# The recurrence head weights' parts in the general tile pool, begun half a slot ahead, and the copies of x moved from the opening to the conv part

## The chip, the core and the metric
One core of a Trainium2 chip. The metric is the device time of one execution in microseconds (us). The kernel before took 731.68 us, the median of three runs from 730.69 to 732.34 us. The profiled execution is a run of its own, with its own time.

## The reference
One layer of a decoder trunk for a sequence of 1024 tokens with 1024 channels, all in fp32:

```python
h = rmsnorm(x, norm_g[l]) * (1.0 + scale[:, None, :]) + shift[:, None, :]
u = h @ w_in[l]                       # conv value, conv gate, conv SiLU gate, lru x, lru gate
v = causal_depthwise_conv(cv * jax.nn.sigmoid(cg), dw_w[l], dw_b[l])      # 31 taps
v = jax.nn.silu(layernorm(v, cln_g[l], cln_b[l]))
y_conv = (v @ pw2_w[l] + pw2_b[l]) * jax.nn.silu(cs)
xs = causal_depthwise_conv(lx, sc_w[l], sc_b[l])                          # 4 taps
...                                   # gates r and i, a, bx: a linear recurrence along the tokens
hs = linear_scan(a, bx)
y_lru = hs * jax.nn.silu(ls)
y = jnp.concatenate([y_conv, y_lru], axis=-1) @ w_out[l]
x = x + (1.0 + gate[:, None, :]) * y
return rmsnorm(x, final_g)
```

shift, scale and gate come from c through a matrix mod_w. `w_out` has 2048 rows: the first 1024 take y_conv, the last 1024 take y_lru. In what follows "lru weights" are those last rows.

## The kernel before, in words
Channels lie on the 128 partitions, tokens along the free axis, so each tensor is eight tiles of 128 x 1024 fp32 (512 KB). A product in fp32 is made from three in the fast fp32r format: an operand w is split in `hi`, its rounded copy, and `lo`, the rest, and the product is hi·hi + hi·lo + lo·hi. Every weight therefore passes three steps before TensorE may use it: a load into a buffer `raw` (SP's queue), a rounding copy `whi` on ScalarE (line 373), and `wlo`. For weights of the early slots `wlo` is a subtraction on GpSimd or VectorE (line 400). For the lru weights it is `remainder` (line 488): ScalarE writes minus `whi` into `wlo` (line 381), and a DMA from GpSimd's queue adds the weight from DRAM onto it (`ADD`, line 403).

The work of TensorE is a row of **slots** n, one per 128 output columns. Slots 4 to 39 are columns of w_in (48 matmuls of 128 x 512 each, written to `ps`, line 525), with eight small gate products between them. Slots 40 to 45 are the lru part of w_out in three **pairs** (`lru_pair`, line 1337): two columns together by a scheme with seven half-size products and the rest straight, with seven letters in `LORDER` for its order. Its matmuls write `lp`, `lx` and `ly` (lines 525 and 1370). Slots 46 and 47 are the last two lru columns, made straight. After them come pw2 (`xpw`, `zpw`, `ypw`, line 694) and the y_conv half of w_out (`xout` and others).

Buffers of 128 x 1024 come from pools. The general pool `big` has NBIG = 47 of them. `raw`, `whi` and `wlo` have pools of their own with two buffers each (lines 345 and 346): a third weight's `whi` has to wait until the first one's matmuls are done. `w_bufs` (line 504) picks the pools.

Nothing is ordered by hand. Every operation is entered in a `Plan` (line 144) with an engine, an estimated cost, the buffers that it reads and writes, and a priority, which for most work is the slot number less or plus something: weights load at n - 2.5 and are prepared at n - 1.4. `Plan.order` (line 206) plays the program through with these costs, and gives each free engine the ready operation of the lowest number whose buffers can be had. The order that comes out is then the program of each engine's queue, and the chip runs each queue in order. An operation with `reserve` is only taken when so many buffers of `big` stay free beside those it needs. `after` orders the plan alone: on the chip only the data's own dependencies are waited for.

The steps that the change and the prediction touch:

- `split` (line 1193) of the recurrence's outputs: `yh` by ScalarE, `yl` by VectorE, priority 38 + 0.2 i, `reserve` SPARE + 1 = 6 for `yh` and 5 for `yl`. They need buffers of `big`, and those come free in slot 39, the last that reads the layer's inputs `uh` and `ul` (two for each of its eight steps k).
- `lru_sums` (line 1267): sums and differences of pairs of those outputs for the scheme, `yhs` and `yls`, at priority 38 + 0.4 j + LTP.
- `lru_prepare` (line 1293): in the opening, sums of lru weights for the scheme (`lz`), made with accumulating DMAs from GpSimd's queue and stored in DRAM.
- `x_copy` (line 1323): nine DMAs from SP's queue that copy x within DRAM to `accd`, 4 MB in all, where the lru part's products are later added (`acc_store`, line 1334, GpSimd's queue). They are entered when n is PREN = 5, with priority XCP = 19.
- `conv_pooled` (line 1126): the depthwise conv of three tiles as a chain of accumulating DMAs from GpSimd's queue (`es<-cq`, `oo<-co`), fed by ScalarE.

Of the kernel before, what the change touches and what calls it, by code (L numbers as in the profile page):

```python
# [14 lines left out]
P = 128  # L15
D = 1024
T = 1024
KT = D // P
# [69 lines left out]
LK = tuple(2 * j + z for z in (0, 1) for j in JS) + tuple(k for k in range(KT) if k // 2 not in JS)  # L88
LACT = ((0, 0), (0, 1), (1, 0), (1, 1))
LORDER = "p1zy2q3s4r"  # L90
LTP = 0.2
LTD = (2,1)
PREN, PRES = 5, 3
PREP, XCP = 18, 19
LEV = ()
QRES = 0
SINGLE = (0,)
AHEAD = 4
# [12 lines left out]
LATE, LAND = 41, 6.0  # L111
# [32 lines left out]
class Plan:  # L144
# [14 lines left out]
    @staticmethod  # L159
    def keys(items):  # L160
        for it in items:
            if isinstance(it, tuple):
                yield it
            else:
                for i in range(it.parts):
                    yield (it, i)
# [162 lines left out]
def hymba_layer(ctx: ExitStack, tc: tile.TileContext, xT, vecs, mod_w, w_first, w_in,  # L329
# [73 lines left out]
    def ADD(prio, out, a, n=T, r=(), w=(), after=(), flight=FLIGHT):  # L403

        return S.op("POOL", ISSUE, lambda: pool.dma_start(out(), a(), accum_op=ALU.add), prio, r,  # L405
                    w, lag=RATE * n / T, after=after, flight=flight)
# [10 lines left out]
    def DMA(prio, out, in_, nbytes, r=(), w=(), after=(), reserve=0):  # L417
        return S.op("SP", max(0.1, nbytes / 360e3),
                    lambda: sp.dma_start(out(), in_()), prio, r, w, after=after,
                    reserve=reserve)  # L420
# [57 lines left out]
    def wsrc(s):  # L478
        if s[0] == "in":
            return w_in[s[1]]  # L480
        if s[0] == "lru":
            return w_out[KT + s[1]]
        return w_out[s[1]] if s[0] == "out" else pw2[s[1]]

    def k3(b):
        return lambda: b().rearrange("p (k c) -> p k c", k=KT)

    def remainder(prio, lo, hi, src, n, rk, wk, sk=(), reserve=0):
        ACT(prio, lo, lambda: hi().bitcast(F32), AF.Copy, n, scale=-1.0, r=rk, w=wk, reserve=reserve)
        ADD(prio, lo, src, n, r=[*wk, *sk], w=wk, flight=LAND)  # L490
# [13 lines left out]
    def w_bufs(s, where=None):  # L504
        n = number[s]
        raw[s] = S.buf("raw", f"raw{n}", F32, KT)
        if where == "all":
            raw[s] = S.buf("big", f"raw{n}", F32, KT)
        whi[s] = S.buf("big" if where else "whi", f"whi{n}", F32R, KT)
        wlo[s] = S.buf("big" if where else "wlo", f"wlo{n}", F32R, KT)  # L510

    def weights(s, after=(), n=None, eng=None, where=None, late=()):
        n = number[s] if n is None else n
        eng = eng or ("DMA" if n in EARLYD or n >= LATE else "POOL" if n < EARLY else "DVE")
        w_bufs(s, where)
        w_slice(s, 0, KT, n - 2.5, n - 1.4, after, eng, late)
# [776 lines left out]
    def lru_prepare(p, after):  # L1293
        w_ = NJ * P
        s0, s1 = wsrc(("lru", 2 * p)), wsrc(("lru", 2 * p + 1))
        z, sh, sl = big_buf(f"lz{p}", parts=4), big_buf(f"lh{p}", F32R), big_buf(f"ll{p}", F32R)

        def block(i):
            return part(z, i * w_, i * w_ + w_)

        def src(w, i):
            return lambda: w[:, i * NJ:i * NJ + NJ, :].rearrange("p k c -> p (k c)")
        load = lambda i, w, k, **kw: DMA(PREP, block(i), src(w, k), P * w_ * 4, w=[(z, i)], after=after, **kw)
        add = lambda i, w, k: ADD(PREP, block(i), src(w, k), w_, r=[(z, i)], w=[(z, i)], flight=LAND)

        def minus(i, k):
            ACT(PREP, block(i), block(k), AF.Copy, w_, scale=-1.0, r=[(z, k)], w=[(z, i)])
        load(3, s1, 0, reserve=PRES)
        minus(0, 3)
        add(0, s0, 0)  # L1310
        add(3, s1, 1)
        minus(2, 0)
        add(2, s1, 1)
        minus(1, 2)
        add(1, s0, 1)
        ACT(PREP, sh, z, "copy", r=[z], w=[sh])
        ACT(PREP, sl, lambda: sh().bitcast(F32), AF.Copy, scale=-1.0, r=[sh], w=[sl])
        ADD(PREP, sl, z, r=[z, sl], w=[sl], flight=LAND)
        for h, t in zip("hl", (sh, sl)):
            s_d[h, p] = dram.tile([P, T], F32, tag=f"ls{h}{p}", name=f"lsd{h}{p}")  # L1320
            DMA(PREP, lambda h=h: s_d[h, p], lambda t=t: t().bitcast(F32), FULL_BYTES, r=[t], w=[("ls", h, p)])
# [15 lines left out]
    def lru_pair(p, n, use, firsts):  # L1337
        rest = LK[2 * NJ:]
        s0, s1 = ("lru", 2 * p), ("lru", 2 * p + 1)
        q = n - 1.4  # L1340
        for s in (s0, s1):
            w_bufs(s)
            DMA(n - 2.5, k3(raw[s]), lambda s=s: wsrc(s)[:, :, :], FULL_BYTES, w=[raw[s]])
        r0, r1 = raw[s0], raw[s1]
        for s, k in ((s0, 0), (s1, NJ)):
            hi, lo, r = whi[s], wlo[s], raw[s]
            cut = lambda b, k=k: (lambda: k3(b)()[:, k:, :])
            keys = lambda b, k=k: [(b, i) for i in range(k, KT)]
            ACT(q, cut(hi), cut(r), "copy", (KT - k) * P, r=keys(r), w=keys(hi))
            remainder(q, cut(lo), cut(hi), lambda s=s, k=k: wsrc(s)[:, k:, :], (KT - k) * P, keys(hi), keys(lo))  # L1350
        def kk(b, i):
            return [(b, k) for k in range(i * NJ, i * NJ + NJ)]

        sh, sl = (big_buf(f"ls{h}{p}", F32R) for h in "hl")
        for h, t in zip("hl", (sh, sl)):
            DMA(n - 2.2, lambda t=t: t().bitcast(F32), lambda h=h: s_d[h, p], FULL_BYTES, r=[("ls", h, p)], w=[t], after=firsts)
        wq = {"S3": (sh, sl, 0, 0), "S4": (sh, sl, 1, 0), "S2": (sh, sl, 2, 0), "S1": (sh, sl, 3, 0),
              "A11": (whi[s0], wlo[s0], 0, None), "A12": (whi[s0], wlo[s0], 1, None),
              "A22": (whi[s1], wlo[s1], 1, None)}
        p0, x, y = mm_tile(f"lp{p}"), mm_tile(f"lx{p}"), acc_tile(f"ly{p}")  # L1360
        g, ops = 0.0, {}

        def quarter(c, a, b, ps, h, begin):
            wh, wl, i, key = wq[a]
            rk = [(wh, key), (wl, key)] if key is not None else kk(wh, i) + kk(wl, i)
            for j, (bh, bl) in enumerate(lsets[b]):
                def emit(j=j, bh=bh, bl=bl):
                    o = (i * NJ + j) * P
                    for lhs, rhs, t in ((wh, bh, 0), (wh, bl, 1), (wl, bh, 2)):
                        pe.matmul(half(ps, h)(), lhs()[:, o:o + P], half(*rhs)(),  # L1370
                                  start=begin and j == 0 and t == 0, stop=j == NJ - 1 and t == 2,
                                  skip_group_check=True)
                o = S.op("PE", 3 * (H + 32) / 2400, emit, n + g, [*rk, bh, bl],
                         [(ps, h if ps.parts > 1 else 0)], columns=3 * H)
                ops.setdefault(c, o)

        for c in LORDER:
            g += 0.12
            if c == "p":
                for k in rest:  # L1380
                    o = mm_k(n + g, p0, s0, yh, yl, k, FULL, first=rest[0])
                    ops.setdefault(c, o)
            elif c == "q":
                for k in rest:
                    mm_k(n + g, y, s1, yh, yl, k, FULL[1:], off=H, first=-1)
                use(n, 1, 1, half(y, 0), (y, 0))
            elif c == "r":
                for k in rest:
                    mm_k(n + g, x, s1, yh, yl, k, FULL[:1], first=-1)
                use(n, 1, 0, half(x, 0), (x, 0))  # L1390
            else:
                a, b, ps, h, begin, i, z = {
                    "1": ("A11", "B11", x, 0, True, 0, 0), "z": ("A12", "B21", p0, 0, False, 0, 0),
                    "2": ("S2", "T2", x, 0, False, 0, 1), "3": ("S3", "T3", x, 0, False, 1, 1),
                    "y": ("S1", "T1", y, 0, True, 0, 1), "s": ("S4", "B22", p0, 1, False, 0, 1),
                    "4": ("A22", "T4", x, 0, False, None, 0)}[c]
                quarter(c, a, b, ps, h, begin)
                if i is not None:
                    use(n, i, z, half(ps, h), (ps, h if ps.parts > 1 else 0))
        return ops["p"], ops["2"]  # L1400
# [67 lines left out]
    for s in slots[4:]:  # L1468
# [23 lines left out]
            n += 1  # L1492
            continue
        if s not in NEXT:
            weights(s, late=[pending_evac[n]] if n in pending_evac else ())
        if GM <= n < GM + 8:
            gate_mod(n - GM, n, [started[n - 2]] if n - 2 in started else [])
        m = s[1]
# [13 lines left out]
        if n == PREN:  # L1512
            for p in range(LRU_P):
                lru_prepare(p, [started[n]])
            for i in range(KT):
                x_copy(i, [started[n]])
        if s[0] == "in":
# [214 lines left out]
```

## Time and profile before

| | before |
|---|---|
| median of 3 runs | 731.68 us |
| profiled execution, its time | 734.07 us |
| its span, first to last instruction | 732.30 us |
| TensorE busy | 719.3 us |
| VectorE, ScalarE, GpSimd busy | 619.9, 479.3, 170.0 us |
| TensorE clock granted, mean | 0.996 |

The profile's page gives each engine's busy time, the span in 40 slices, the chain of work that ended last, and the costliest groups. Besides the page the trace answers to views: who waited for whom, the instructions of one engine in order of time, busy times by stretch of the span, and the DMA queues. In a row of the timeline stand the start and the duration in us, the engine, the line, the operation, what it writes and reads, and in brackets the idle time just before with what ended it. Buffer numbers are left out: `wlo` stands for every weight's rest.

### The profile page before, as it was taken

To read this page: it belongs to the slowest core of one execution; us is meant where nothing else is said; L and a number is where in the kernel's file an instruction comes from. 1 tells how busy PE (TensorE), PEld (TensorE's weight loads), DVE (VectorE), ACT (ScalarE), POOL (GpSimd) and SP (SyncE) were. 2 spreads that over 40 slices of the span, in tenths; PEclk is the share of its full clock that TensorE was granted. 3 is DMA by queue.
4 is the path that set the end of the run, shared out by engine and by line. 5 is a ranking of instruction groups with operands and counts; after the bars stand their busy time and mean duration, and the time that the engine had idled before them with its cause. 6 is when DMAs were issued, how large, how long until landed. Compare 5 with 4: busy or idle time off the path is not lost.

```text
span 732.3 us, 9063 instructions
## 1 busy us (share of the span) xinstructions
PE 719.3 (98%) x3274; PEld 597.4 (82%) x3274; DVE 619.9 (85%) x848; ACT 479.3 (65%) x614; POOL 170.0 (23%) x172
## 2 busy tenths in 40 slices
PE   9999999999999999999999999999999999999996
PEld 8888878888888888888888888787877888888885
DVE  7999999999789998688499995998897556999646
ACT  7650589565689767957949869757793345755322
POOL 0035223343534230233220220111111001010003
PEclk9999999999999999999999999999999999999998
DMA  9946838758898997899893695998577845784006
GB/s 340 407 154 204 240 102 232 200 116 200 181 221 201 266 234 200 183 226 207 191 198 73 134 208 137 265 247 213 108 142 157 230 118 132 219 216 181 15 15 215
DMA packets 46059, 137.80 MB, mean 188 GB/s; under 512 B 5200, under 2 KB 15824, under 8 KB 45904
## 3 DMA queue, kind: packets, MB, share of 16 engines
q0 software_dynamic: 20016, 54.84, 41.8%
q1 hardware_dynamic: 24992, 81.48, 31.9%
q10 hardware_dynamic: 1008, 0.92, 0.4%
q8 instruction: 25, 0.41, 0.2%
q14 instruction: 18, 0.15, 0.1%
HBM read 79.37 MB, written 21.50 MB: 138 GB/s over the span
## 4 chain that ended last, share of the span: by engine, by line
PE 74%; DVE 11%; DMA 6%; ACT 4%; issue 3%; SPq 0%; POOL 0%; DVEq 0%; ACTq 0%; POOLq 0%
PE ps L525 38%; PE xout L694 6%; PE xpw L694 6%; PE first L821 5%; PE ypw L694 3%; PE gate L1241 3%; DMA lz<-in_w_out_dram 3%; DMA wlo<-in_w_out_dram 2%; DVE caccs L392 2%; PE y L669 2%; PE zout L694 1%; PE zpw L694 1%; PE lp L525 1%; PE lx L1370 1%; DMA wlopw<-in_pw_dram 1%
## 5 line engine op out<-in xcount | busy, mean ns | idle before, releaser
L525 PE MATMUL ps<-ul,whi 128*128 128x512 f32 x576 | 177.5, 389 | 0.5 <-DVE ul L392 0.5
L525 PE MATMUL ps<-uh,whi 128*128 128x512 f32 x576 | 177.4, 389 | 0.0
L525 PE MATMUL ps<-uh,wlo 128*128 128x512 f32 x576 | 177.4, 389 | 0.0
L525 PEld LDWEIGHTS ps<-ul,whi 128*128 128x128 f32 x576 | 108.1, 188 | 23.3 <-DVE ul L392 0.9
L525 PEld LDWEIGHTS ps<-uh,wlo 128*128 128x128 f32 x576 | 108.1, 188 | 22.4
L525 PEld LDWEIGHTS ps<-uh,whi 128*128 128x128 f32 x576 | 108.0, 188 | 22.5
L373 ACT CAST whi<-raw 128x1024 fp32r<-128x1024 f32 (+1 forms) x44 | 45.2, 1032 | 44.1 <-PE ps L525 30.5
L405 POOL DMA_DIRECT2D es<-cq x45 | 40.6, 903 | 136.0 <-ACT cq L381 77.4
L400 POOL TENSOR_TENSOR wlo<-raw,whi 128x1024 fp32r<-128x1024 f32 x16 | 40.8, 2558 | 85.2 <-ACT whi L373 85.1
L381 ACT ACT_TABLE_LOAD x44 | 56.5, 1283 | 5.5 <-issue 3.0
L392 DVE SCALAR_TENSOR_TENSOR cacc<-v,V,cacc 128x511 f32<-128x511 f32 (+14 forms) x75 | 55.5, 741 | 0.5
L392 DVE SCALAR_TENSOR_TENSOR caccs<-v,V,caccs 128x511 f32<-128x511 f32 (+6 forms) x70 | 52.1, 744 | 2.2 <-ACT caccs L381 1.1
L392 DVE SCALAR_TENSOR_TENSOR caccs<-c,wsum,caccs 128x511 f32<-128x511 f32 (+6 forms) x70 | 52.0, 742 | 0.8
L405 POOL DMA_DIRECT2D oo<-co x39 | 36.7, 972 | 44.5 <-issue 14.4
L381 ACT ACTIVATE cq<-v,V 128x511 f32<-128x511 f32 (+14 forms) x45 | 31.7, 707 | 0.0
L392 DVE SCALAR_TENSOR_TENSOR xs<-ps,V,xs 128x1023 f32<-128x1023 f32 (+2 forms) x24 | 30.6, 1276 | 0.0
L381 ACT ACTIVATE cq<-c,wsum 128x512 f32<-128x512 f32 x42 | 29.6, 711 | 0.0
L392 DVE SCALAR_TENSOR_TENSOR modw<-modw,sc 128x1024 f32<-128x1024 f32 x23 | 29.5, 1285 | 0.0
L400 DVE TENSOR_TENSOR wlo<-raw,whi 128x1024 fp32r<-128x1024 f32 x20 | 24.4, 1219 | 5.2 <-ACT whi L373 5.0
L381 ACT ACTIVATE co<-v,V 128x510 f32<-128x510 f32 (+12 forms) x39 | 26.9, 705 | 0.0
L381 ACT ACTIVATE finsq<-fin 128x512 f32<-128x512 f32 (+2 forms) x14 | 7.8, 569 | 26.5 <-PE xout L694 13.2
L373 ACT CAST xsh<-xs 128x1024 fp32r<-128x1024 f32 x8 | 8.4, 1052 | 24.2 <-issue 14.8
(413 smaller groups left out, 1593.1 us busy)
## 6 DMA issues: line engine op xcount, KB each, us to landing
raw<-in_w_in_dram SPq DMA_DIRECT2D x36, 512.0 KB, 6.0
modw<-in_mod_w_dram SPq DMA_DIRECT2D x24, 512.0 KB, 9.3
scsd<-scs SPq DMA_DIRECT2D x8, 512.0 KB, 4.5
raw<-in_w_out_dram SPq DMA_DIRECT2D x8, 512.0 KB, 4.3
accd<-acc POOLq DMA_DIRECT2D x8, 512.0 KB, 6.2
rawpw<-in_pw_dram SPq DMA_DIRECT2D x8, 512.0 KB, 4.4
scsr<-scsd SPq DMA_DIRECT2D x8, 512.0 KB, 5.0
rawout<-in_w_out_dram SPq DMA_DIRECT2D x8, 512.0 KB, 3.8
```

Source lines behind the costliest of these rows:

```text
L373: act.copy(out(), in_())
L381: act.activation(out=out(), in_=in_(), func=func, **kw)
L392: dve.scalar_tensor_tensor(out=out(), in0=in0(), scalar=scalar, in1=in1(), op0=op0, op1=op1, accum_out=accum)
L400: lambda: e.tensor_tensor(out=out(), in0=a(), in1=b(), op=op), prio, r, w,
L405: return S.op("POOL", ISSUE, lambda: pool.dma_start(out(), a(), accum_op=ALU.add), prio, r, w, lag=RATE * n / T, after=after, flight=flight)
L525: pe.matmul(ps()[:, a - off:b - off], k3(lhs)()[:, at, :], rhs[k]()[:, a:b], start=(k == first and lhs is wh and rhs is xh and (a - off) % ...
L669: pe.matmul(to(), half(*lhs)()[:, j * P:j * P + P], half(*rhs)()[:, c0:c1], start=a == "S1" and j == 0 and t == 0, stop=j == KT // 2 - 1 a ...
L694: pe.matmul(half(ps, 0)(), half(*lhs)()[:, j * P:j * P + P], half(*rhs)(), start=start and j == 0 and t == 0, stop=j == KT // 2 - 1 and t ...
L821: pe.matmul(ps()[:, a - off:b - off], fw_part(lhs, k, i * P, i * P + P)(), rhs()[:, a:b], start=k == 0 and lhs is wh and rhs is xh, stop=k ...
L1241: pe.matmul(ps()[:, c0:c1], lhs()[:, j, :], rhs()[:, c0:c1], start=st == 0, stop=st == 2)
L1370: pe.matmul(half(ps, h)(), lhs()[:, o:o + P], half(*rhs)(), start=begin and j == 0 and t == 0, stop=j == NJ - 1 and t == 2, skip_group_che ...
```

## The change
The parts `whi` and `wlo` of the lru weights come from the pool `big` in place of their own two-buffer pools (`LWB`); `raw` stays where it was. Their loads and preparations get priorities 0.5 lower (`LWO`), so that they are begun half a slot earlier. The priority number of `lru_sums` grows by 0.3 (`LTP`), so they come later among ready operations. The copies of x are entered in slot XCN = 33 in place of 5, with the same priority 19. `PLAND` takes the place of `LAND` in `lru_prepare` with the same value 6.0, and `LRV`, by which a weight's rest could be made on VectorE, is empty.

```diff
-LTP = 0.2
+LTP = 0.5
+PLAND = 6.0
+XCN = 33
+LWB = "big"
+LWO = 0.5
+LRV = ()
...
-        q = n - 1.4
+        q = n - 1.4 - LWO
         for s in (s0, s1):
-            w_bufs(s)
-            DMA(n - 2.5, k3(raw[s]), lambda s=s: wsrc(s)[:, :, :], FULL_BYTES, w=[raw[s]])
+            w_bufs(s, LWB)
+            DMA(n - 2.5 - LWO, k3(raw[s]), lambda s=s: wsrc(s)[:, :, :], FULL_BYTES, w=[raw[s]])
...
-            remainder(q, cut(lo), cut(hi), lambda s=s, k=k: wsrc(s)[:, k:, :], (KT - k) * P, keys(hi), keys(lo))
+            if s[1] in LRV:
+                SUB(q, "DVE", cut(lo), cut(r), cut(hi), (KT - k) * P, r=keys(r) + keys(hi), w=keys(lo))
+            else:
+                remainder(q, cut(lo), cut(hi), lambda s=s, k=k: wsrc(s)[:, k:, :], (KT - k) * P, keys(hi), keys(lo))
...
         if s not in NEXT:
-            weights(s, late=[pending_evac[n]] if n in pending_evac else ())
+            if s[0] == "lru":
+                weights(s, n=n - LWO, eng="DVE" if s[1] in LRV else "DMA", where=LWB)
+            else:
+                weights(s, late=[pending_evac[n]] if n in pending_evac else ())
...
         if n == PREN:
             for p in range(LRU_P):
                 lru_prepare(p, [started[n]])
+        if n == XCN:
             for i in range(KT):
                 x_copy(i, [started[n]])
```

More of the change, by code (lines that the diff above doesn't have):

```diff
@@ L1303, in lru_prepare @@
         load = lambda i, w, k, **kw: DMA(PREP, block(i), src(w, k), P * w_ * 4, w=[(z, i)], after=after, **kw)
-        add = lambda i, w, k: ADD(PREP, block(i), src(w, k), w_, r=[(z, i)], w=[(z, i)], flight=LAND)
+        add = lambda i, w, k: ADD(PREP, block(i), src(w, k), w_, r=[(z, i)], w=[(z, i)], flight=PLAND)
         def minus(i, k):
@@ L1317, in lru_prepare @@
         ACT(PREP, sl, lambda: sh().bitcast(F32), AF.Copy, scale=-1.0, r=[sh], w=[sl])
-        ADD(PREP, sl, z, r=[z, sl], w=[sl], flight=LAND)
+        ADD(PREP, sl, z, r=[z, sl], w=[sl], flight=PLAND)
         for h, t in zip("hl", (sh, sl)):
```

## The prediction
> **What bounds the kernel now.** I read the page first, then the view of who waited for whom, for TensorE (PE) alone.
>
> ```profile
> span 732.3 us, 9063 instructions
> PE 719.3 (98%) x3274; PEld 597.4 (82%) x3274; DVE 619.9 (85%) x848; ACT 479.3 (65%) x614; POOL 170.0 (23%) x172
> ```
>
> ```profile
> PE ly L525 <- DMA wlo<-in_w_out_dram: 1.5, 1, 1.5
> PE xpw L694 <- DMA wlopw<-in_pw_dram: 1.5, 1, 1.5
> PE token_stats L778 <- DVE ones L450: 1.1, 1, 1.1
> PE finbc L743 <- DVE rs65.7_0_5820 L752: 0.9, 1, 0.9
> PE lx L1370 <- DMA wlo<-in_w_out_dram: 0.6, 1, 0.6
> PE lx L1370 <- DVE acc L392: 0.5, 1, 0.5
> PE ps L525 <- DVE ul L392: 0.5, 1, 0.5
> ```
>
> PE is the bound from end to end. The change takes no matmul away, so it can win only PE's idle time, 732.3 - 719.3 = 13.0 us, most of it the start and the tail, which it does not touch. Of the seven waits above, the first belongs to a pair of lru columns, the fifth too; both wait for the accumulating DMA that finishes a `wlo`. The second is pw2's first product, right behind the lru part. What each takes from PE is read from the timeline, from one start to the next:
>
> ```profile
> 472.46 0.39 PE L1370 MATMUL lx<-yl,whi 128*128 128x512 f32 x1
> 473.49 0.50 PE L1370 MATMUL lx<-yh,wlo 128*128 128x512 f32 x1 [0.65 <-DMA wlo<-in_w_out_dram]
> 473.83 0.39 PE L525 MATMUL lp<-yh,whi 128*128 128x512 f32 x1
> ...
> 505.61 0.39 PE L525 MATMUL ly<-yl,whi 128*128 128x512 f32 x1
> 507.51 0.50 PE L525 MATMUL ly<-yh,wlo 128*128 128x512 f32 x1 [1.51 <-DMA wlo<-in_w_out_dram]
> 507.85 0.39 PE L525 MATMUL ly<-yh,whi 128*128 128x512 f32 x1
> ...
> 536.49 0.39 PE L1370 MATMUL lp<-yh,lsl 128*128 128x512 f32 x1
> 537.41 0.50 PE L1370 MATMUL lx<-yhs,whi 128*128 128x512 f32 x1 [0.53 <-DVE acc L392]
> ...
> 552.51 0.62 PE L525 MATMUL ps<-yh,whi 128*128 128x512 f32 x2
> 563.39 0.39 PE L694 MATMUL xpw<-vha,whipw 128*128 128x512 f32 x1
> 563.62 0.39 PE L694 MATMUL xpw<-vla,whipw 128*128 128x512 f32 x1
> 565.50 0.50 PE L694 MATMUL xpw<-vha,wlopw 128*128 128x512 f32 x1 [1.50 <-DMA wlopw<-in_pw_dram]
> 565.84 0.39 PE L694 MATMUL xpw<-vha,whipw 128*128 128x512 f32 x1
> ```
>
> Undisturbed, starts lie 0.23 us apart (563.39 to 563.62). Around the first wait two steps take 1.03 and 0.34 us, so it costs 1.03 + 0.34 - 0.46 = 0.91. In the same way the second costs 1.90 + 0.34 - 0.46 = 1.78, and pw2's 1.88 + 0.34 - 0.46 = 1.76. The wait for DVE's `acc` at 537.41 costs 0.92 - 0.23 = 0.69, and some 0.1 after it. The step from 552.51 to 563.39 is a whole slot, 10.88 us, or 1.36 for each of its eight steps k.
>
> **Part 1, the pool of the weights' parts.** What made these three `wlo` late:
>
> ```profile
> 461.10 1.06 ACT L373 CAST whi<-raw 128x1024 fp32r<-128x1024 f32 x1 [3.86 <-PE ps L525]
> 482.67 1.05 ACT L373 CAST whi<-raw 128x1024 fp32r<-128x1024 f32 x1 [1.93 <-PE lp L1370]
> 495.60 0.82 ACT L373 CAST whi<-raw 128x768 fp32r<-128x768 f32 x1
> ...
> 553.56 1.05 ACT L373 CAST whipw<-rawpw 128x1024 fp32r<-128x1024 f32 x1
> ```
>
> ```profile
> 464.68 8.77 DMA wlo<-in_w_out_dram
> ...
> 498.51 8.95 DMA wlo<-in_w_out_dram
> ...
> 556.50 8.96 DMA wlopw<-in_pw_dram
> ```
>
> ```profile
> 441.29 0.33 SPq L419 DMA_DIRECT2D raw<-in_w_out_dram  x1
> ```
>
> The first pair's weight was loaded from 441.29, but its rounding copy at 461.10 ended an idle stretch of 3.86 us that PE's slot 38 released: a buffer of the two-buffer pool came free. From 461.10 to the landing at 464.68 + 8.77 = 473.45 it is 12.35 us, and PE wanted it at 472.69 (472.46 + 0.23). The third row, 495.60, is the second pair's second weight; the pair before held its buffer to its end. It landed at 498.51 + 8.95 = 507.46 and was wanted at 505.84 (505.61 + 0.23). With `whi` and `wlo` in `big`, neither copy waits for these matmuls. The first can stand in the 3.86 us of idle ScalarE time or before it; 0.8 us earlier is enough, and half a slot (5.44 us) is what the priorities ask for. The second needs 1.7 us, and the same pair's first copy stands 12.9 us ahead of it, at 482.67, so there is room. **Both waits go: -0.91 - 1.78 = -2.69 us.** What is late next is a wait for DVE's evacuations, as at 537.41; it costs 0.8 us there already.
>
> The pw2 copy at 553.56 also came right after slot 46 had ended (552.51), and with it the hold on a `whi` buffer. After the change the two-buffer pools are empty from slot 39's end, so it can be made as soon as its weight is there. Two ends: -1.76 when the wait goes, 0 when the DMA keeps its place in GpSimd's queue, since there it stands behind a store that waits for a product:
>
> ```profile
> 555.85 0.86 POOL L405 DMA_DIRECT2D accd<-acc  x1 [9.21 <-DVE acc L414]
> ```
>
> GpSimd issues in order: with the copy planned earlier its `ADD` has 9.21 us of idle queue to go into. I take -1.76, since 1.66 us earlier is enough.
>
> **What it costs: buffers.** Up to eight more buffers of `big` are held. Counted from the code at slot 39: `uh` and `ul` 16, the eight outputs `sls`, `yh` and `yl` of two heads 4, conv tiles 5, their sums `csum`, `es`, `oo`, one `v`, `lsh` and `lsl`, and a few passing ones: about 42 of 47. A `yh` split needs seven free, so it may start at 40 held or fewer. Those splits feed slot 40:
>
> ```profile
> 463.92 1.98 ACT L373 CAST yh<-sls 128x1024 fp32r<-128x1024 f32 x2
> ...
> 475.58 1.99 ACT L373 CAST yh<-sls 128x1024 fp32r<-128x1024 f32 x2
> ```
>
> The first pair's four new buffers make the splits wait for two more steps k of slot 39, 2 x 1.36 = 2.72 us. Against that ScalarE loses the two rounding copies and their negatives from this stretch, some 1 us each. Nothing in the trace shows the squeeze itself. Ends: 0 (PE has other products of the pair to take first) and 2.72. I take the middle step, **+1.36 us**, because the splits end at 477.57, when PE already works in that pair: they have no time to spare. `LTP` moves two groups of sums behind the splits that are needed first; its cost is in that term, with the same ends.
>
> **Part 2, the copies of x.** They leave the opening and come to slot 33, that is to about 390 us.
>
> ```profile
> accd<-in_xT_dram SPq DMA_DIRECT2D x7, 512.0 KB, 10.2
> ```
>
> ```profile
> 66.00:88.00 22.00, 22.00 (x106) 18.48 (x105) 21.69 (x46) 7.89 (x15) 4.36 (x5) 1.00 0.93 266
> ...
> 388.00:404.00 16.00, 16.00 (x72) 13.27 (x71) 15.79 (x22) 15.72 (x17) 0.14 (x1) 1.00 0.36 79
> ```
>
> The columns are the stretch, its length, the busy time of PE, PEld, DVE, ACT and POOL, the clock, the DMA engines' share and GB/s. In the opening PE ran without a gap in that stretch, so taking nine DMAs away wins at most the wait for `ul`, 0.5 us; I take 0. At the new place the DMA engines are 0.36 busy at 79 GB/s. At the opening's 266 GB/s, 4 MB written and as much read lie between 4.2 / 0.266 = 16 and 32 us of DMA time, beside what is there. Two things share it:
>
> ```profile
> 404.51 0.86 POOL L405 DMA_DIRECT2D es<-cq  x1 [16.37 <-ACT cq L381]
> 413.14 1.04 ACT L373 CAST whi<-raw 128x1024 fp32r<-128x1024 f32 x1
> ```
>
> ```profile
> L419 SPq DMA_DIRECT2D raw<-in_w_in_dram x4: 327/327/328, 393.6 to 428.7; - x4
> ```
>
> GpSimd's queue, which drives the conv chain, waited 16.37 us there for ScalarE. On SP's queue the weight load at 393.6 now stands behind nine issues; it is not rounded before 413.14, 19.5 us later. So I cost the move at **0**. If the copies held the load for all of 32 us, it would come 32 - 19.5 = 12.5 us late, and that is the far end; 0 is taken because the nearer 16 us is under the 19.5.
>
> A rule speaks against the move. The Trainium skill (DMA: Bandwidth & Descriptors, Issuing engines are not separate DMA queues) says that DMAs of all issuing engines run on the same 16 and interleave, so the copies would slow GpSimd's conv adds wherever they are put. By it the sum would be the same only while the 16.37 us cover holds.
>
> **The sum.** -2.69 - 1.76 + 1.36 + 0 = -3.09 us. The profiled execution, 734.07 us (span 732.30), would become 730.98 (span 729.21). It is 2.39 us above the median of the runs, 731.68, from which the same step gives **728.6 us**, -0.42%. A measurement of this kernel tells about 0.2% from no change, 1.46 us.
>
> **The rivals.**
> (a) As forecast, 728.6: chance 0.46. Its own range is 725.9 to 730.0: from all waits gone with no squeeze (-2.69 - 1.76 - 0.8 for `acc` - 0.5 for `ul`) to the squeeze at 2.72 (-1.73).
> (b) pw2's wait stays, as GpSimd's queue keeps its order: -2.69 + 1.36 = -1.33, 730.4 us. For it speaks the 9.21 us wait in front of that store; against it that the copy has no buffer to wait for. Chance 0.12.
> (c) The change does not do what it says: `raw` still has two buffers and GpSimd's queue still mixes `wlo` with `accd` stores that wait for products, so the `wlo` come no sooner: 731.7. Against it stands the load at 441.29, 20 us before its copy. Chance 0.10.
> (d) Slower: `big` runs out at slot 40. The weights' priority lets the second pair's parts, which ask for no reserve, take buffers that the last `yh` splits need with seven free. The splits then wait until the first pair's parts come free, which the trace places at 482.67 (the copy that PE's `lp` released), in place of 475.58: 7.09 us. PE runs dry by that much less the products it can bring forward. Without any of those: 731.68 - 4.45 + 7.09 = 734.3 us. It decides against the change from a stall of 4.45 + 1.46 = 5.9 us on; at 2.7 to 5.9 it eats the gain. For it speaks the count of 42 of 47; against it that PE's order is planned with it. Chance 0.32.
>
> Beside (d) a page has a price of its own: the Trainium skill (TensorE: Matmul & The Clock Gate, What's actually happening) says that an idle window of about 3.4 us halves TensorE's clock. The row of 388.00 above has the clock at 1.00, and no wait of PE here is longer than 1.5 us, so no run here shows it in mid-kernel. By the page (d) would be later by an estimated 1.7 us.
>
> **The numbers.** Faster by over 0.2%: (a) and a third of (b), which lies close to that bound, 0.50. Within 0.2%: the rest of (b) and (c), 0.18. Slower: (d), 0.32, and in it 0.03 for the far end of the copies. The range of 8 in 10 goes from 726.2 to 734.6: it leaves out 0.05 below and about 0.15 of (d) above.
>
> **What would show it.** Right: no PE wait on `wlo<-in_w_out_dram`, rounding copies of lru weights without PE as releaser, no `accd<-in_xT_dram` before 380 us, `wlopw`'s DMA issued before 553, and PE's idle time at slot 40 under 1.4 us. Wrong: waits of `lx`, `lp` or `ly` on ACT `yh` or DVE `yl` near 470 to 490, which is (d); a PE wait on `wlo<-raw` near 410, which is part 2; or a wait on the conv's normalisation behind slot 47, if `big` also holds up its splits.

## The result, and the profile after

The changed kernel takes 729.72 us, the median of 11 runs from 728.43 to 731.08. The kernel before, on the same chip, takes 732.34 us, the median of 11 runs from 730.69 to 734.53. The ratio is 0.9964, with a 95% interval of 0.9952 to 0.9976: faster by 0.36%, where 0.42% was forecast. The medians differ by 2.62 us, where 3.09 was forecast. The forecast of 728.6 us started from 731.68 us, the median of three runs; the 11 runs beside the changed kernel lie 0.66 us higher, which is more than half of the 1.12 us by which the forecast is off.

The page of the kernel after, its span and the busy times:

```profile
span 728.7 us, 9085 instructions
PE 718.4 (99%) x3274; PEld 597.2 (82%) x3274; DVE 616.9 (85%) x848; ACT 481.7 (66%) x615; POOL 171.0 (23%) x172
```

The profiled execution took 730.56 us (forecast 730.98), its span 728.7 (forecast 729.21). PE does the same 3274 matmuls. The engines' busy times have hardly moved; the 3.6 us between the two profiled executions (a run each, so not the 2.62 of the medians) come from the gaps between matmuls. The waits of PE in the kernel after (total, times, longest, in us):

```profile
PE token_stats L783 <- DVE ones L455: 1.1, 1, 1.1
PE finbc L748 <- DVE rs65.7_0_5820 L757: 0.9, 1, 0.9
PE xout L699 <- DMA wloout<-in_w_out_dram: 0.8, 1, 0.8
PE lx L1378 <- DVE acc L397: 0.5, 1, 0.5
PE zpw L699 <- DVE vlb L405: 0.4, 1, 0.4
PE lp L530 <- DVE yl L405: 0.3, 1, 0.3
```

Beside the list of before, both waits for `wlo` are gone, so is pw2's for `wlopw`, and so is the opening's for `ul`. Three are new: `lp` for a `yl`, `zpw` for `vlb`, `xout` for `wloout`. What they cost is read from the starts in PE's timeline, as before (0.23 us is an undisturbed step, 0.46 one of a row with x2):

```profile
473.90 0.61 PE L530 MATMUL lp<-yh,whi 128*128 128x512 f32 x2
474.81 0.73 PE L530 MATMUL lp<-yl,whi 128*128 128x512 f32 x2 [0.29 <-DVE yl L405]
475.38 0.62 PE L530 MATMUL lp<-yh,wlo 128*128 128x512 f32 x2
...
478.35 0.39 PE L1378 MATMUL lx<-yhs,lsl 128*128 128x512 f32 x1
478.83 0.50 PE L530 MATMUL ly<-yh,whi 128*128 128x512 f32 x1
479.17 0.40 PE L530 MATMUL ly<-yl,whi 128*128 128x512 f32 x1
...
564.57 0.39 PE L699 MATMUL zpw<-vhb,whipw 128*128 128x512 f32 x1
565.39 0.50 PE L699 MATMUL zpw<-vlb,whipw 128*128 128x512 f32 x1 [0.43 <-DVE vlb L405]
565.73 0.40 PE L699 MATMUL zpw<-vhb,wlopw 128*128 128x512 f32 x1
...
649.49 0.39 PE L699 MATMUL xout<-yla,whiout 128*128 128x512 f32 x1
650.67 0.50 PE L699 MATMUL xout<-yha,wloout 128*128 128x512 f32 x1 [0.79 <-DMA wloout<-in_w_out_dram]
651.00 0.40 PE L699 MATMUL xout<-yha,whiout 128*128 128x512 f32 x1
```

The `yl` wait costs 0.91 + 0.57 - 0.92 = 0.56 us, the gap before `ly` 0.48 + 0.34 - 0.46 = 0.36: 0.92 at slot 40. In that gap PE's weight load waited 0.52 us for ScalarE's `acc`, the evacuation of `ly`. `vlb` costs 0.82 + 0.34 - 0.46 = 0.70, `wloout` 1.18 + 0.33 - 0.46 = 1.05. ScalarE's timeline of the kernel after, its rounding copies and the end of the `yh` splits:

```profile
450.63 1.99 ACT L378 CAST whi<-raw 128x1024 fp32r<-128x1024 f32 x2
460.74 0.82 ACT L378 CAST whi<-raw 128x768 fp32r<-128x768 f32 x1
...
466.50 1.06 ACT L378 CAST yhs<-sls 128x1024 fp32r<-128x1024 f32 x1 [1.22 <-DMA es<-cq]
...
478.68 1.04 ACT L378 CAST yh<-sls 128x1024 fp32r<-128x1024 f32 x1
...
481.67 0.82 ACT L378 CAST whi<-raw 128x768 fp32r<-128x768 f32 x1
...
544.63 1.04 ACT L378 CAST whipw<-rawpw 128x1024 fp32r<-128x1024 f32 x1
```

No lru weight's copy ends an idle stretch released by PE any more. The first pair's first copy is done by 452.62, against a start at 461.10 before; the second pair's second at 481.67, against 495.60; pw2's at 544.63, against 553.56. The price is in the third row. ScalarE stood for 1.22 us until a DMA of the conv chain had landed. `yhs` is made from `sls` and reads nothing of that DMA, so what it waited for must have been a buffer; `cq`, which the DMA reads, is one of `big`. The `yh` split behind it came at 471.50, and VectorE made from it the `yl` that PE waited for:

```profile
473.54 2.35 DVE L405 TENSOR_TENSOR yl<-sls,yh 128x1024 fp32r<-128x1024 f32 x2
```

The last `yh` split starts at 478.68, where the last two started from 475.58, but PE had brought other products forward and did not wait for it.

### The profile page after: what moved, and what is told of

The parts are those of the page before. It is cut to its first block, busy times and chain, and to the rows that moved or that the text cites. A ratio compares the mean times of both kernels' runs of the same rounds, so it can differ in the third digit from the quotient of the medians.

```text
span 728.7 us, 9085 instructions
## 1 busy us (share of the span) xinstructions
PE 718.4 (99%) x3274; PEld 597.2 (82%) x3274; DVE 616.9 (85%) x848; ACT 481.7 (66%) x615; POOL 171.0 (23%) x172
## 4 chain that ended last, share of the span: by engine, by line
PE 81%; issue 6%; DVE 5%; ACT 4%; DMA 2%; POOL 1%; DVEq 0%; POOLq 0%; ACTq 0%
PE ps L530 49%; PE xout L699 5%; PE first L826 5%; PE xpw L699 5%; PE ypw L699 3%; PE gate L1246 2%; PE y L674 2%; PE lp L530 1%; DMA wloout<-in_w_out_dram 1%; PE zpw L699 1%; DMA accd<-acc 1%; PE zout L699 1%; PE lx L1378 1%; ACT L386 1%; PE yout L699 1%
## 5 line engine op out<-in xcount | busy, mean ns | idle before, releaser
L405 POOL TENSOR_TENSOR o<-fin,bc 128x256 f32<-128x256 f32 (+1 forms) x8 | 7.8, 997 | 70.6 <-ACT bc L378 70.6
```

The lines of the kernel that those rows point to most:

```text
L405: lambda: e.tensor_tensor(out=out(), in0=a(), in1=b(), op=op), prio, r, w,
```

## The experiments

Each kernel is the changed one with the edit shown, unless it says otherwise. Ratios are to the kernel before on the same chip. The runs of one group shared a chip: the first four, the next four and the last four.

### One part of the change alone

**The copies of x alone.** All else as before: the parts in their own pools, no earlier start, the old LTP.

```diff
-LTP = 0.5
+LTP = 0.2
-LWB = "big"
-LWO = 0.5
+LWB = None
+LWO = 0.0
```

> Only the copies of x are moved to slot 33; pools, the half slot and LTP as before. Theory A (each part has its own share: the pool frees the wlo, the copies free the opening's accumulating DMAs): the gaps of PE in the opening go (0.72 at slot 7, 0.37 at the first gate), and the waits for wlo at slots 40 and 43 and for wlopw stay: 1.1 to 1.5 us faster than before. Theory C (the prediction's 0 for the copies: the opening's gaps are the scheduler's luck and come or go with any new order): within 0.5 us of before, or opening gaps of another size.

734.98 us, ratio 1.001 (0.9989 to 1.003): nothing that can be measured. The wait for `ul` in the opening is gone, but the waits for `wlo` and `wlopw` stay, 0.9 us for `wloout` and 0.4 us for a `yl` have come, and the longest wait for a `wlo` is followed by something new. PE's timeline of this kernel:

```profile
505.08 0.39 PE L530 MATMUL ly<-yl,whi 128*128 128x512 f32 x1
507.51 0.79 PE L530 MATMUL ly<-yh,wlo 128*128 128x512 f32 x1 [2.04 <-DMA wlo<-in_w_out_dram]
508.11 0.63 PE L530 MATMUL ly<-yh,whi 128*128 128x512 f32 x1
508.53 0.63 PE L530 MATMUL ly<-yl,whi 128*128 128x512 f32 x1
...
510.67 0.51 PE L530 MATMUL ly<-yh,whi 128*128 128x512 f32 x1
511.01 0.39 PE L530 MATMUL ly<-yl,whi 128*128 128x512 f32 x1
```

Behind the wait of 2.04 us the starts lie 0.42 to 0.43 us apart in place of 0.23, until 510.67. Eight steps take 511.01 - 507.51 = 3.50 us, 1.7 us more than the 1.8 that they take undisturbed. In the kernel before, behind 1.51 us at the same place, that did not happen.

**The pool alone.** The copies stay in the opening, no earlier start, the old LTP.

```diff
-LTP = 0.5
-XCN = 33
-LWO = 0.5
+LTP = 0.2
+XCN = PREN
+LWO = 0.0
```

> Only the pool of the lru weights' parts is changed; copies in the opening, no half slot, LTP 0.2. Theory A: no PE wait on wlo at slots 40 to 47, pw2's wait on wlopw gone or replaced by a smaller one on the normalisation's splits, a wait of 0.5 to 1.5 us for yl at slot 40, the opening's gaps as before: 2 to 3 us faster than before. Theory B (starting half a slot sooner is what makes the wlo come in time; the pool alone is not needed): the waits of 0.65 and 1.51 us on wlo stay, same time as before.

730.83 us, ratio 0.9962 (0.9945 to 0.9979): as much as the whole change gains, with neither the copies nor the earlier start. No wait for `wlo` or `wlopw` is left; `yl` (0.7 us in two waits) and `vlb` (0.7 us) have come in their place.

**All but the pool.**

```diff
-LWB = "big"
+LWB = None
```

> The changed kernel with the weights' parts back in their two-buffer pools; half a slot, LTP 0.5 and the copies' new place stay. Theory A: the waits of PE on wlo return, 0.9 and 1.8 us, and wlopw's 1.8; the opening's gaps stay gone; so about 1.1 to 1.5 us faster than before. Theory B: no wait on wlo, and the time of the changed kernel, 2.6 us below before.

736.69 us, ratio 1.0059 (1.0035 to 1.0083): slower than before. PE's waits in this kernel:

```profile
PE xpw L699 <- DMA wlopw<-in_pw_dram: 2.1, 1, 2.1
PE ly L530 <- DMA wlo<-in_w_out_dram: 1.6, 1, 1.6
PE lx L1378 <- DVE acc L397: 1.2, 1, 1.2
```

The earlier start brings nothing without a buffer: the waits are still there and longer than before (1.5 us each). (LTP and the copies are changed here too. The copies alone took 1.001; what LTP adds by itself was not run.) Behind the 2.1 us the clock falls again; from 567.4 to 570.8 us the matmuls' starts lie 0.42 us apart.

### Where the squeeze sits

**The first pair back in its own pools.**

```diff
-            w_bufs(s, LWB)
+            w_bufs(s, LWB if p else None)
```

> The changed kernel, but the first pair's parts (slots 40, 41) stay in their own two-buffer pools; the other lru weights are in the general pool. Theory A (four fewer buffers held while the outputs are split, at the price of the hold by slot 38): the yl waits at slot 40, 0.58 and 0.36 us, go, and the wait for the first wlo, 0.91 us, comes back: within 0.5 us of the changed kernel. Rival (the buffers are not what delays yl; ScalarE's and VectorE's own order is): the yl wait stays and the wlo wait comes on top: 0.9 us slower than the changed kernel.

729.64 us, ratio 0.9941 (0.9914 to 0.9968). The `yl` wait and the `vlb` wait are gone, a `wlo` wait of 0.84 us at slot 40 is back: squeeze and first wait trade places.

**Only the first pair's second weight back.**

```diff
-            w_bufs(s, LWB)
+            w_bufs(s, LWB if p or s is s0 else None)
```

> The changed kernel, but of the first pair only the first weight's parts (slot 40) are in the general pool; the second's (slot 41), for which TensorE never waited, stay in their own pools. Theory A (each of the two buffer effects is local: the hold by slot 38 delays only the first wlo, and buffers held while the outputs are split delay only yl): no wait on wlo, the yl wait of 0.58 us smaller or gone, so 0.5 to 1.5 us below the changed kernel and 3 to 4.5 us below before. Rival (any two buffers fewer or more merely reshuffle the plan): other waits of the same sum, within 0.5 us of the changed kernel.

728.74 us, ratio 0.9955 (0.9942 to 0.9967). Besides `token_stats` at the start and `finbc` in the tail PE waits once in this kernel. The row, and ScalarE's last `yh` split:

```profile
PE mean L1427 <- ACT csh L378: 0.5, 1, 0.5
```

```profile
473.08 1.05 ACT L378 CAST yh<-sls 128x1024 fp32r<-128x1024 f32 x1
```

With two buffers of `big` fewer in use ScalarE's wait of 1.22 us is gone, the split of the `yl` in question comes at 470.23 in place of 471.50, the last one at 473.08 in place of 478.68, and the waits for `yl` and `acc` and the gap before `ly` go, with no wait for a `wlo` in return. ScalarE waits in this way, 1.2 to 1.4 us at a `yhs` or `yls` until `es<-cq` has landed, in the profiles of the changed kernel, of the pool alone and of the pairs alone (below), and 9 us in the one with the copies in slot 38 (below). These hold both weights of the first pair in `big`. In the others with the reserve of 5 it does not. So the squeeze belongs to those two buffers. They are not the whole order: with the copies alone PE waits 0.4 us for a `yl` too, and here the last split is earlier than even before the change (475.58). The median is 1.0 us below the 729.72 of the changed kernel, which was measured on another chip; the last group has both on one.

### What makes pw2's wait

**Only slots 46 and 47 in the general pool.**

```diff
-            w_bufs(s, LWB)
+            w_bufs(s)
```

> The changed kernel with the three pairs' parts back in their own pools; only the last two lru weights (slots 46, 47) are in the general pool. Theory A (the hold is local): waits for wlo at slots 40 and 43 return (0.9 and 1.8 us), wlopw's wait before pw2 does not, since the two-buffer pools are empty from the third pair's end: about 0.5 to 1.5 us faster than before. Rival (pw2's wait is set by GpSimd's queue, not by the buffer): wlopw's wait of 1.5 us stays, same time as before.

731.01 us, ratio 0.9982 (0.9965 to 0.9999). The two `wlo` waits of the pairs are back (0.62 and 1.44 us), pw2's is gone.

**Only the pairs in the general pool.**

```diff
-                weights(s, n=n - LWO, eng="DVE" if s[1] in LRV else "DMA", where=LWB)
+                weights(s, n=n - LWO, eng="DVE" if s[1] in LRV else "DMA", where=None)
```

> The changed kernel with the last two lru weights back in their own pools; the three pairs' parts are in the general pool. Theory A: no wait for wlo at slots 40 and 43, the wait for wlopw before pw2 is back at 1.5 to 2.1 us, and the wait for vlb there (0.70 us) goes, since four fewer buffers are held while the normalised conv is split: within 1 us of the changed kernel, 1 to 2 us faster than before. Rival (pw2's wait is set by GpSimd's queue): no wait for wlopw, 0.5 us faster than the changed kernel.

728.81 us, ratio 0.9949 (0.9926 to 0.9972). No wait for `wlo`, and none for `wlopw` either, though slots 46 and 47 hold the two buffers of their own pools again. (The wait for `vlb` is gone, as expected; one of 1.2 us for a `uh` in the opening has come, and `wloout` and `yl` still cost waits of 0.6 and 0.3 us.) Both edits take pw2's wait away, so a hold on a `whi` buffer cannot be its whole cause.

**The first pair's second weight and slots 46 and 47 in their own pools**, both edits at once:

```diff
-            w_bufs(s, LWB)
+            w_bufs(s, LWB if p or s is s0 else None)
...
-                weights(s, n=n - LWO, eng="DVE" if s[1] in LRV else "DMA", where=LWB)
+                weights(s, n=n - LWO, eng="DVE" if s[1] in LRV else "DMA", where=None)
```

> The first pair's second weight and the two straight columns (slots 46, 47) have their parts in their own two-buffer pools again, all other lru weights' parts stay in the general pool. Theory (each hold of a buffer acts only at its own place, so the two cures add): no PE wait on a wlo of the pairs, none on yl near 475, none on vlb near 565, and no wait on pw2's wlopw, whose copy then follows the end of slot 46 within 1 us and lands within one slot: 0.993 to 0.996 of before, within 1 us of the kernel with only the first weight's exception. Rival (the plan's order is what pays, and any further edit reshuffles it): waits over 1 us at some other place, 0.996 to 1.000.

728.96 us, ratio 0.9946 (0.9926 to 0.9966), and pw2's wait is back. Its chain in this kernel, from ScalarE's, GpSimd's and PE's timelines, and the time from that DMA's issue to its landing:

```profile
548.28 1.06 ACT L378 CAST whipw<-rawpw 128x1024 fp32r<-128x1024 f32 x1 [1.57 <-PE ps L530]
```

```profile
551.08 0.86 POOL L410 DMA_DIRECT2D accd<-acc  x1 [9.91 <-DVE acc L419]
551.73 1.13 POOL L410 DMA_DIRECT2D wlopw<-in_pw_dram  x1
```

```profile
560.87 0.50 PE L699 MATMUL xpw<-vha,wlopw 128*128 128x512 f32 x1 [0.84 <-DMA wlopw<-in_pw_dram]
```

```profile
DMA to landing us min/median/max: 9.1/9.1/9.1
```

The copy was held until slot 46's end, as the prediction had it. In the kernel before, the row just ahead of the copy at 553.56 says something else:

```profile
552.60 1.05 ACT L373 CAST vhc<-vt 128x1024 fp32r<-128x1024 f32 x1 [4.04 <-DVE vt L400]
```

ScalarE stood there for VectorE's `vt`, and the copy came behind it; that this was just after slot 46's end does not show a hold. The held buffer may have set that order in the plan; no run shows it. And the kernel with only the first weight's exception issued the same DMA later than the one here, and did not wait. GpSimd's timeline and the landing there:

```profile
552.76 0.88 POOL L410 DMA_DIRECT2D wlopw<-in_pw_dram  x1 [12.90 <-issue]
```

```profile
DMA to landing us min/median/max: 5.1/5.1/5.1
```

What differs is the flight. In the five kernels where this DMA was issued directly behind an `accd` store, at most 1.2 us after it, it flew 9.0 us (before), 9.2 (the copies alone), 9.1 (here), 7.5 (all but the pool) and 6.8 (only the pairs). In six others, where no store was issued just ahead, it flew 5.1 to 5.4 us; the changed kernel is one of them, with 5.3 in both of its profiles. In these runs pw2's wait came only with both: a copy at or after slot 46's end, and a store just ahead in GpSimd's queue. (With only the pairs in the general pool both were there too, but the copy followed slot 46 at once and 6.8 us were just short enough.) The late copy alone makes no wait. Whether a store just ahead would make one behind an early copy is open: an early copy's DMA was always issued before that store.

### The reserve, and the copies of x without cover

**A smaller reserve**, so that splits may take the last buffers of `big`:

```diff
-SPARE = 5
+SPARE = 2
```

> The changed kernel with the reserve that the outputs' splits must leave free cut from 5 buffers to 2. Rival (d) of the prediction, that the general pool runs out near slot 40 and PE then waits for buffers, is pushed to its end: the splits take what the second pair's weights and the sums need, and PE stands still near slot 40 for more than 6 us, the time is over 5 us above before. If the pool has room to spare here, the splits come 1 to 2 us earlier, the yl wait goes and the time is that of the changed kernel or 1 us less.

809.81 us in one run, 77 above the median of before. PE's waits in this kernel:

```profile
PE lnbc L742 <- DVE lnss L405: 17.9, 1, 17.9
PE mean L1427 <- ACT csh L378: 12.0, 1, 12.0
PE lp L530 <- DMA wlo<-in_w_out_dram: 10.4, 1, 10.4
```

With three buffers less in reserve the later conv and its normalisation come late (the first two rows), and a `wlo` by 10.4 us; before that `wlo` ScalarE had stood 8.50 us for a DMA of the conv chain. The same reserve holds for the sums `yhs` and `yls`. This is a stall that the reserve had kept away, but not the one of rival (d), in which the weights take the buffers and the splits wait: here the splits and the sums may take more, and the conv and the weights wait. `big` has little room.

**The copies of x in slot 38.**

```diff
-XCN = 33
+XCN = 38
```

> The copies of x entered in slot 38 in place of 33, so that they stand at about 450 us beside the loads and the accumulating DMAs of the first pair's weights, the rest as in the changed kernel. Theory (at slot 33 the copies are free because the weight load behind them had 19.5 us and GpSimd's conv chain was waiting for ScalarE; at 38 they share the DMA engines with wlo): wlo's accumulating DMA of the first pair takes over 9 us, a PE wait on wlo or raw of 1 to 10 us near slot 40 comes up, 1 to 6 us above the changed kernel. Rival (the copies cost nothing anywhere, the DMA engines have room): no new PE wait, within 1.5 us of the changed kernel.

746.87 us in one run, where the changed kernel took 728.38 to 730.88 us on that chip: 17 us slower. PE's waits and a piece of the chain of waits in this kernel (start, us, what):

```profile
PE lp L530 <- ACT yh L378: 5.3, 1, 5.3
PE mean L1427 <- ACT csh L378: 3.1, 1, 3.1
PE lp L530 <- DVE yl L405: 2.0, 1, 2.0
```

```profile
460.06 15.63 DMA es<-cq
```

```profile
475.77 1.04 ACT L378 CAST yhs<-sls 128x1024 fp32r<-128x1024 f32 x1 [9.02 <-DMA es<-cq]
```

The expectation had the price right in kind and the victim wrong: the first pair's `wlo` fly 10.3 and 12.4 us, over 9 as expected, but none is late. One accumulating DMA of the conv chain, issued while the copies ran, took 15.63 us; ScalarE's next instruction waited 9.02 us for it, and the `yh` splits behind it in ScalarE's queue came too late for PE. Behind each wait the clock fell, so the loss is more than the 10.4 us of waits. Not all of the 15.63 us is the copies' doing: that DMA was issued 0.57 us behind a `wlo`, and in the pool-alone kernel, where it stands 0.57 us behind a `wlo` too and the copies are in the opening, it flew 9.4 us. And ScalarE's wait is the squeeze again, a `yhs` that wants a buffer: the copies in slot 38 were not run with the first pair's second weight in its own pools, where no such wait was seen.

The same DMA shows why slot 33 is free. The view of the tile `es` from 382 to 388 us, in the kernel before and then after:

```profile
L405 POOL DMA_DIRECT2D es<-cq x1: 872/872/872, 386.4 to 386.4; - x1
DMA to landing us min/median/max: 4.6/4.6/4.6
```

```profile
L410 POOL DMA_DIRECT2D es<-cq x1: 869/869/869, 385.0 to 385.0; - x1
DMA to landing us min/median/max: 13.1/13.1/13.1
```

Beside the copies, issued from 377.7 to 383.7, it flew 13.1 us in place of 4.6. In nine profiles with the copies in slot 33 the DMA in this place flew 10.0 to 13.3 us, in four with the copies elsewhere 4.6 to 4.9. But behind it and its neighbour `oo<-co`, which landed by 400.3, GpSimd's queue stood idle for 16.40 us, until ScalarE's `cq` let the next one go at 403.14, and in that stretch no engine waited for it.

**The copies back in the opening, in the best version**: the first pair's second weight in its own pools, and the old LTP.

```diff
-LTP = 0.5
+LTP = 0.2
-XCN = 33
+XCN = PREN
...
-            w_bufs(s, LWB)
+            w_bufs(s, LWB if p or s is s0 else None)
```

> The first pair's second weight in its own pools, the copies of x left in the opening and LTP at 0.2, the rest as in the changed kernel. Theory (the copies are worth nothing that can be measured wherever they stand, only their gaps of 0.37 us at the gate products come and go): within 1 us of the same kernel with the copies in slot 33, 0.993 to 0.997 of before, with the two gaps near 118 and 438 us back. Rival (the copies out of the opening carry part of the gain): 1.5 us or more above it, 0.997 to 0.999.

728.70 us, ratio 0.9942 (0.992 to 0.9964). The list of PE's waits holds only `token_stats` and `finbc`, the start and the tail. Of the two gaps expected back, the one near 438 us is there (0.37 us), the one near 118 is not, and nor is the wait for `ul`. So those gaps do not hang on the copies, and the copies' place is worth nothing here.

**The changed kernel again**, on the chip of the last group:

> The changed kernel itself, to stand beside the others on one chip. All theories: 0.995 to 0.998 of before. If the squeeze and the vlb wait are real losses, it is 0.7 to 2 us above the kernel with the first pair's second weight in its own pools; if those waits only trade places, the two are alike.

729.90 us, 11 runs from 728.38 to 730.88, ratio 0.9958 (0.9943 to 0.9972), with the same new waits in its profile (`wloout` 0.8, `vlb` 0.6, `yl` 0.3). The two kernels beside it with the first weight's exception took 728.96 (728.47 to 730.54) and 728.70 (728.16 to 729.64): about 1 us less, as the squeeze would have it, though the intervals of the ratios overlap.

## Why the prediction was right, point by point

- **The first `wlo`, -0.91, and the second, -1.78.** Both as predicted, by the mechanism predicted: the buffer held them, not the load and not the priority. The pool alone gives it, the earlier start without the pool does not.
- **pw2's `wlopw`, -1.76.** The wait went, but the hold on a `whi` buffer, which the step gives as the cause, is by the runs not enough. The step read the copy at 553.56 as held by slot 46, and set the order of GpSimd's queue against it as rival (b). The row ahead of that copy has ScalarE standing for VectorE, a late copy alone makes no wait, and each wait had a store just ahead in GpSimd's queue. After the change the copy comes 8.9 us earlier and the DMA at 547.81, ahead of the store, where the step asked for 1.66 us (1.61 by its own rows: landed 565.46, wanted 563.85). That it came out is in part luck: with only the pairs in the general pool the copy was as late as slot 46's end, and the wait went all the same. What is late next the step did not price, though the list of signs has it (a wait on the conv's normalisation): at 565.39 `zpw` waits 0.43 us for `vlb`; it costs 0.70 us, so the place nets -1.06. VectorE had come behind at an earlier `vlb`; its timeline of the kernel after:

```profile
548.50 1.23 DVE L405 TENSOR_TENSOR vlb<-c,vhb 128x1024 fp32r<-128x1024 f32 x1 [2.59 <-DMA accd<-acc]
```

  What it waited for is a store of an `acc`, of which it reads nothing, so its new buffer had held that `acc`. From there to the late `vlb` at 564.12 it worked without a pause. The pool-alone kernel has this wait too, and in each of the six kernels where some of the parts went back to their own pools it is gone, so the fuller `big` is paid for here as well; by what path was not shown.
- **The squeeze, +1.36.** Measured 0.92, inside the bounds of 0 and 2.72. The squeeze is there by the predicted way, buffers of `big` that come free late: ScalarE stood 1.22 us for one. It falls on `yl`, 0.56. The rest, 0.36 before `ly`, is a wait for ScalarE's evacuation, which went with the squeeze when the two buffers were given back. The wait was for a DMA of the conv chain and not for steps k of slot 39, as the term has it, and the last split, which does come late, cost nothing. That the price belongs to the first pair's second weight the prediction could not say.
- **The copies, 0.** Right for the result. The cover taken from the trace was the right one: GpSimd's conv chain had 16 us of idle time, of which the slowed DMAs left 2.8. The far end of +12.5 was sized on the wrong victim: it counted on the weight load behind the copies, and without cover the conv chain's DMA loses; the run with slot 38, with the order that the plan gave it, lost 17 us. The rule cited there (the Trainium skill, DMA: Bandwidth & Descriptors, Issuing engines are not separate DMA queues) agrees with the 4.6 and 13.1 us: copies from SP's queue slow GpSimd's DMAs.
- **What the sum lacked.** Three small gaps left, 0.72 for `ul` and twice 0.37 at the gate products, together -1.46; one came, +1.05 for `wloout`. Without copies in the opening the changed kernel has none of the three, but the run with the copies back there and the run with them in slot 38 show that they come and go with the whole order. The sum -2.69 - 1.06 + 0.92 - 1.46 + 1.05 = -3.24 stands against -3.09 predicted and -3.6 in the spans; the rest lies at the start and the tail. The medians give -2.62. That the sum is so close is in part luck: the terms that it lacked come to -0.41, pw2's step was 0.70 too good and the squeeze 0.44 too dear.
- **The rivals.** (b) has the store that makes pw2's DMA slow, but not the time. (c) fell with the pool-alone run; the two copies that still wait, at 509.17 and 514.57, wait for their load, and PE does not wait for them. (d) did not come up as a stall. What was named as its sign, a wait of `lp` on a `yl` near 475, came all the same, with 0.56 us: the sign does not part (d) from the squeeze that the sum had priced. The run with the smaller reserve shows a stall of another kind and so no price for (d).
- **The signs.** Of those for being right, one failed by a little: the copies were issued from 377.7 us, not after 380. It changes nothing in the sum.

Open is why `wloout` lands late. Its DMA flew 9.3 and 10.2 us in the two profiles of the changed kernel, 10.6 with the copies alone, 8.0 before and 7.9 with the first weight's exception, but also 9.1 without a wait with the copies back in the opening; no run tells what it shared the DMA engines with.

## What to carry to other kernels

When a weight's first preparation step ends an idle stretch that the matmuls release, the buffer is late and not the load: look for a pool with room before you move priorities, since an earlier start without a buffer brought nothing here (with the copies' move and LTP it was 0.6% slower). Count what the larger pool then lacks, and give the extra buffers to those weights alone that waited (about 1 us here, at the edge of what the runs can tell). Put a bulk copy where the queue that shares the DMA engines with it is idle for longer than its DMAs are slowed: the same nine copies cost nothing in slot 33, and the kernel with them in slot 38 was 17 us slower.

## What the runs showed of the hardware

TensorE's clock fell behind waits that seemed too short for it. Behind 2.04 us (the copies alone) and 2.09 us (all but the pool) some 3 us of matmuls went at about half speed (0.42 to 0.43 us a step in place of 0.23), at once in the first and from 1.5 us later in the second, and the mean granted clock was 0.89 from 505 to 520 us and 0.91 from 560 to 580 us. Behind the waits of 1.4 to 1.83 us, in four kernels, it stayed at 1.00. With the first pair in its own pools the clock was 0.89 from 505 to 520 us with no wait over 0.3 us there, but with sixteen matmuls of one column just ahead, which stand in every kernel here; the sixteen of 128 columns behind them took 3.55 us, where they took 1.95 in every other kernel but the one with the smaller reserve, in which a long wait stood just ahead. The Trainium skill (TensorE: Matmul & The Clock Gate, What's actually happening) gives an idle window of about 3.4 us, which runs freely, so that the moment of the step varies. The traces agree that it varies; that so long a window must be idle they do not bear out. The prediction left the clock out of all but rival (d), and by these runs a wait of some 2 us can be enough.

The flight of pw2's first `wlopw`, an accumulating DMA of 512 KB, went with what was issued just ahead of it: 5.1 to 5.4 us with no store there, 6.8 to 9.2 right behind one of the same size. This is not a rule for all such DMAs. The first pair's `wlo` in the kernel before, at 464.68, flew 8.8 us with nothing from GpSimd's queue in the 7 us ahead of it, though SP's queue had issued three DMAs in the 2.5 us ahead; and in the changed kernel one issued at 518.02 flew 8.5 us with nothing from GpSimd's queue in the 6 us ahead but another `wlo`, 3.0 us before it. What else slows them no run here parts.
